# Output stage of a hybrid decoder layer: product order 7, 1, 6, 5, 3, 2, 4 with shared banks, three w_out sums made earlier, all sums on VectorE

## The chip, the cores and the metric

The kernel runs on one core of a Trainium2 chip. The metric is the device time of one execution in microseconds. The kernel before takes 1931.66 us, the median of three runs (1928.71 to 1932.95). The inputs are one sequence of 1024 tokens with a model width of 2048, in fp32.

## The reference

One layer, cut to its steps; `concat` is 2048 wide, and so is the output.

```python
h = rms_norm(x, norm_gain) * (1 + scale) + shift        # (1024, 2048)
proj = h @ w_in                                         # (2048, 8192): q k v z twice
oa = stick_breaking_attention(rms(qa), rms(ka), va) * silu(za)   # 8 heads of 128
ob = head_group_norm(chunkwise_retention(rotary(qr), rotary(kr), vr)) * silu(zr)
y = concatenate([oa, ob], -1) @ w_out                   # (2048, 2048)
out = x + gate * y
```

`scale`, `shift` and `gate` come from silu(c) @ w_ada + b_ada. The change concerns the last product, `concat @ w_out`, and what happens beside the input projection.

## The kernel before

**Arithmetic.** Every fp32 operand is cut in two: a high part (ScalarE's copy, L173 or L181) and a low part (VectorE's subtraction of the high part, L175 or L182). `mm3` then issues three matmuls for one product, high by high, high by low, low by high (L186 to L188). Both large products use Strassen's scheme in Winograd's form: 7 products of quarter matrices in place of 8, with sums of quarters ahead of and behind them.

**Groups.** The input projection runs in seven groups (0 to 6), each of 7 products in the order T4, B11, T2, T1, B22, B21, T3 (in groups 1 and later), named after their right factor. The left operands (`A`, w_in) are loaded raw (L260), summed on VectorE (L296) and cut (L173, L175); the right factors were cut once, in group 0, lie in DRAM (`fac`), and come back through a ring of buffers (L273, L275). One product of a group takes some 28 us. Between the matmuls of the projection small generators run a step at each tick: stick-breaking attention beside groups 1 to 4, retention beside groups 5 and 6, and two that only prepare something, `gate_steps` and `bias_steps` (the latter yields 6 ticks and 2 ticks in turn for each of its loads).

**Output stage** (L1424 and behind). The left matrix is `concat` turned (features by tokens), the right one w_out; each quarter product gives 512 by 1024 results, which is 4 token tiles by 2 halves of 512 columns `m`, and so all 8 PSUM banks, one tile `y` each. The inner dimension has 8 chunks `k` of 128. `steps` lists (product, halves, k): product 1 goes first with one half at a time (16 steps), then 7, 2, 6, 5, 3, 4 with both halves (8 steps each), 64 steps in all. A step has 24 matmuls (12 in the first 16 steps); the steps k=6 and k=7 of a product are issued together, bank by bank, and behind each bank the generator `later(1, ...)` puts its evacuation `evac_o` (L1618 to L1656). What multiplies results by the gate and adds x waits in a queue `fin`, from which one or two operations are taken at a time. Ahead of a step i, the right quarters of step i+6 are loaded (`load_right`), those of step i+5 summed where a product needs a sum (`sum_right`, GpSimd, L1474), and those of step i+3 cut. Sums of left quarters (`left_sum`, L1504 to L1516) stand on GpSimd as well. T3 (of product 7) and T2 (of product 6) are stored to DRAM once made (`sums_o`, L1483), and loaded again for the product behind (`load_s`, L1441).

**Order.** All of it runs in the order in which it is written out. SP issues every load and every store in that order, so a store that waits for its result holds back the loads behind it. The four evacuations of a product with most work are those of 6 and 5, L1628 and L1629, and L1631 to L1643; those of 3 are L1646 and the `fin` operations L1609 and L1613; those of 4 are L1653 and L1654.

Of the kernel before, what the change touches and what calls it, by code (L numbers as in the profile page):

```python
# [17 lines left out]
P = 128  # L18
# [80 lines left out]
def layer_kernel(ctx, tc, x, c, w_ada, b_ada, norm_gain, w_in, sb_q_gain, sb_k_gain, ret_norm_gain, w_out,  # L99
# [21 lines left out]
    sums_o = {(n, k): dr.tile([P, S], F32, name=f"sum_{n}_{k}") for n in ("T3", "T2") for k in range(8)}  # L121
# [729 lines left out]
    def bias_steps():  # L851

        acc = {}
        for i in range(2):
            n = min(HALF, NZ * P - i * HALF)
            acc[i] = get(f"qb_acc{i}", "att", borrow=True)
            for kc in range(KC):
                raw = get(f"wb_{kc}_{i}", "att", borrow=True)
                nc.sync.dma_start(raw[:, 0:n], w_in[0][kc * P:(kc + 1) * P, rqcol + i * HALF:rqcol + i * HALF + n])
                yield 6  # L860
                a, r, by = acc[i][:, 0:n], raw[:, 0:n], shift[:, kc:kc + 1]
# [6 lines left out]
        while clock[0] < scored[0] + 2:  # L868
            yield 1
        zs = ps.tile([P, NZ], F32, tag="A0", name="zs")  # L870
        for h in range(NZ):
            nc.tensor.matmul(zs[:, h:h + 1], acc[h // 4][:, h % 4 * P:(h % 4 + 1) * P], ones[:, 0:1],
                             start=True, stop=True)
        nc.vector.tensor_copy(qb[:, 0, 0:NZ], zs)
        put(acc[0], acc[1])
        yield 2
        nc.scalar.activation(qb[0:64, 1, 0:NZ], qb[64:128, 0, 0:NZ], AF.Copy)
        nc.scalar.activation(qb[64:128, 1, 0:NZ], qb[0:64, 0, 0:NZ], AF.Copy)
# [53 lines left out]
    def next_bank():  # L932
        turn_of[0] += 1
        return ("A0", "A1", "B", "C")[turn_of[0] % 4]

# [488 lines left out]
    steps = [(1, (m,), k) for m in range(2) for k in range(8)]  # L1424
    steps += [(prod, (0, 1), k) for prod in (7, 2, 6, 5, 3, 4) for k in range(8)]
    rraw, rcut, lraw, lcut, X, Y, gates, xrs = {}, {}, {}, {}, {}, {}, {}, {}
# [23 lines left out]
    def load_right(i):  # L1450
# [15 lines left out]
    def sum_right(i):  # L1466

        if i >= len(steps):
            return
        prod, ms, k = steps[i]  # L1470
        for m in ms:
            if len(rraw[i, m]) == 2:
                a, b = rraw[i, m]
                nc.gpsimd.tensor_tensor(a, a, b, op=ALU.add if prod == 6 else ALU.subtract)  # L1474
                put(b)

    def cut_right(i, m):
        if i >= len(steps) or m not in steps[i][1]:
            return
        prod, ms, k = steps[i]  # L1480
# [6 lines left out]
    def cut_left(i):  # L1487
# [3 lines left out]
        b = {1: "A11", 7: "S3", 2: "A12", 6: "A11", 5: "A21", 3: "A12", 4: "A22"}[prod]  # L1491
        t = lraw.pop(k) if prod == 7 else A_[b][k]
        lcut[i] = split(t, f"l{i}")
        if prod in (7, 5, 3, 4):
            put(t)
# [7 lines left out]
    def left_sum(n, k):  # L1503

        if n == "S3":
            t = lraw[k] = anywhere(f"S3o_{k}")
            nc.gpsimd.tensor_tensor(t, A_["A11"][k], A_["A21"][k], op=ALU.subtract)
        elif n == "S1":
            nc.sync.dma_start(concat[8 + k][:, halves(1)], A_["A22"][k])
            nc.gpsimd.tensor_tensor(A_["A21"][k], A_["A21"][k], A_["A22"][k], op=ALU.add)  # L1510
            put(A_["A22"].pop(k))
        elif n == "S2":
            nc.gpsimd.tensor_tensor(A_["A11"][k], A_["A21"][k], A_["A11"][k], op=ALU.subtract)
        else:
            nc.gpsimd.tensor_tensor(A_["A12"][k], A_["A12"][k], A_["A11"][k], op=ALU.subtract)
            put(A_["A11"].pop(k))  # L1516
# [18 lines left out]
    LOADS, SUMS, CUTS = 6, 5, 3  # L1535
    for k in range(8):
        at(6 + k, load_a, "A21", k)
        at(11 + k, left_sum, "S3", k)
        at(16 + k, load_a, "A12", k)
        at(19 + k, times_z, "A12", k)  # L1540
        at(18 + k, load_a, "A22", k)
        at(21 + k, times_z, "A22", k)
        at(22 + k, left_sum, "S1", k)
        at(27 + k, left_sum, "S2", k)
        at(33 + k, left_sum, "S4", k)
# [11 lines left out]
    for j in range(len(entries)):  # L1557
# [25 lines left out]
        if 3 <= left_over <= 8:  # L1583
            load_a("A11", 8 - left_over)
            load_right(8 - left_over)
        if left_over <= 3:
# [19 lines left out]
    def queue_out(t, n, y_):  # L1606

        load_xr(t, n)
        fin.append(lambda: nc.vector.tensor_tensor(y_, y_, gates[n], op=ALU.mult))  # L1609
# [8 lines left out]
    def evac_o(prod, b, o):  # L1618
        if prod in (1, 7):
# [3 lines left out]
        elif prod == 2:  # L1623
            y_ = anywhere(f"yt_{prod}_{b}")
            nc.vector.tensor_tensor(y_, o, X[b], op=ALU.add)
            queue_out(*where(prod, b), y_)
        elif prod == 6:
            nc.vector.tensor_tensor(X[b], o, X[b], op=ALU.add)  # L1628
            later(1, lambda: nc.vector.tensor_tensor(Y[b], X[b], Y[b], op=ALU.add))  # L1629
        elif prod == 5:  # L1630
            nc.vector.tensor_tensor(X[b], o, X[b], op=ALU.add)  # L1631
            y_ = anywhere(f"yt_{prod}_{b}")
            nc.vector.tensor_tensor(y_, o, Y[b], op=ALU.add)
            queue_out(*where(prod, b), y_)
            t, n = where(4, b)
            load_xr(t, n)
            fin.append(lambda: nc.vector.tensor_tensor(Y[b], Y[b], gates[n], op=ALU.mult))

            def add_x():
                x_ = xrs.pop((t, n))  # L1640
                nc.vector.tensor_tensor(Y[b], Y[b], x_, op=ALU.add)
                put(x_)
            fin.append(add_x)  # L1643
        elif prod == 3:
            y_ = X.pop(b)
            nc.vector.tensor_tensor(y_, o, y_, op=ALU.add)  # L1646
            queue_out(*where(prod, b), y_)
        else:
            y_, (t, n) = anywhere(f"yt_{prod}_{b}"), where(prod, b)
            for i, eng in enumerate((nc.sync, nc.scalar) if b == 7 else (nc.sync,)):  # L1650
# [3 lines left out]
                nc.vector.tensor_tensor(y_[:, sl], y_[:, sl], Y[b][:, sl], op=ALU.add)  # L1654
                eng.dma_start(out[0][t * P:(t + 1) * P, n * HALF + i * w:n * HALF + (i + 1) * w], y_[:, sl])
            put(y_, Y.pop(b))  # L1656
# [29 lines left out]
    for i, (prod, ms, k) in enumerate(steps):  # L1686
# [8 lines left out]
        for d in range(2 if both else 1):  # L1695
            load_right(i + d + LOADS)
            sum_right(i + d + SUMS)
            if i + d < 2:
                load_a("A11", i + d + LOADS)
# [24 lines left out]
        for d in range(2 if both else 1):  # L1724
            lcut.pop(i + d)
# [55 lines left out]
```

## Time and profile before

| | |
|---|---|
| median of three runs | 1931.66 us (1928.71 to 1932.95) |
| the profiled execution: its own time | 1935.53 us |
| the profiled execution: its span | 1933.8 us |
| granted TensorE clock, mean over the span | 0.993 |
| output stage, first matmul of `y` to the end of the span | 1598.8 to 1933.8 us |
| GpSimd, busy over the span | 254.4 us of 1933.8, 374 instructions |

The span is what the profile sees of the execution; its own time is 1.7 us longer. The profiled execution lies 3.9 us above the median. In a table of windows each row is a stretch of the span: first its length, then the busy time of PE, PEld (TensorE's weight loads), DVE (VectorE), ACT (ScalarE) and POOL (GpSimd) with the number of instructions in brackets, then the TensorE clock that was granted (1.00 is full), the busy share of the DMA engines and GB/s. A matmul of 512 columns shows 0.39 us in the records, but one starts every 0.227 us: the records overlap, so that a busy time near the window's length says little, and the number of matmuls in a window says more. The same holds for VectorE, whose records of 0.68 us start 0.60 us apart. A row of a timeline has the start, the duration, the engine, the line, the result and its operands, and in square brackets the idle time ahead of it and what ended that.

### The profile page before, as it was taken

The page shows a single profiled execution, that of the slowest core. Times are in us where ns is not written, and L with a number is a line of the kernel's source. Part 1 is how long each engine was busy: PE and PEld are TensorE (multiplying, and loading weights), DVE is VectorE, ACT ScalarE, POOL GpSimd, SP SyncE. Part 2 cuts the span into 40 slices and gives each one's busy share as a digit, 9 for nine tenths or more (in the row PEclk, how much of TensorE's full clock was granted, in tenths as well). Part 3 has the DMA queues.
Part 4 walks back from the last instruction along what each step waited for, and adds up shares of the span by engine and source line. Part 5 has one row for each costly group of instructions (what it writes and reads, how often), then busy time and mean ns, then how long its engine had stood idle before and what let it go on. Part 6 is the DMA issues. An engine that isn't in the chain of part 4 may idle for free.

```text
span 1933.8 us, 28606 instructions
## 1 busy us (share of the span) xinstructions
PE 1877.2 (97%) x9511; PEld 1538.1 (80%) x9511; DVE 1377.4 (71%) x2522; ACT 839.7 (43%) x1574; POOL 254.4 (13%) x374
## 2 busy tenths in 40 slices
PE   5999999999999999999999999999999999998988
PEld 3777778878788878887888788888888888886777
DVE  4637765447768777877787667966786657898797
ACT  5437852234544454445444444333343546422221
POOL 0000000000110011001000100000000003597232
PEclk9999999999999999999999999999999999999999
DMA  9969996897798779977997788989988847988574
GB/s 319 361 206 315 322 339 244 284 354 250 245 302 281 255 255 318 312 259 241 310 299 260 255 264 277 296 255 315 343 290 243 273 144 255 327 295 278 161 254 160
DMA packets 407216, 532.62 MB, mean 275 GB/s; under 512 B 33566, under 2 KB 207000, under 8 KB 407068
## 3 DMA queue, kind: packets, MB, share of 16 engines
q1 hardware_dynamic: 406536, 530.62, 83.2%
q8 instruction: 75, 1.23, 0.3%
q14 instruction: 73, 0.60, 0.1%
q10 hardware_dynamic: 532, 0.17, 0.0%
HBM read 444.64 MB, written 86.02 MB: 274 GB/s over the span
## 4 chain that ended last, share of the span: by engine, by line
PE 42%; DVE 6%; DMA 3%; issue 1%; SPq 0%; ACT 0%; POOL 0%; DVEq 0%; POOLq 0%
PE pj L186 8%; PE pj L188 8%; PE pj L187 8%; PE y L186 3%; PE y L187 3%; PE y L188 3%; DMA wB<-in_w_out_dram 1%; PE op L1321 1%; PE sp L1305 1%; PE op L1323 1%; PE up L1287 1%; DVE wl_l L175 1%; DVE r_1l L182 0%; DVE Y L1629 0%; DVE yt L1609 0%
## 5 line engine op out<-in xcount | busy, mean ns | idle before, releaser
L175 DVE TENSOR_TENSOR wl<-A,wh 128x512 fp32r<-128x512 f32 x392 | 272.1, 694 | 274.9 <-ACT wh L173 251.8
L173 ACT ACTIVATE wh<-A 128x512 fp32r<-128x512 f32 x392 | 246.7, 629 | 358.9 <-PE pj L187 341.7
L1086 POOL TENSOR_SCALAR_AFFINE_SELECT om<-om 128x128 f32<-128x128 f32 x64 | 25.5, 398 | 1073.8 <-ACT om L1083 936.6
L389 ACT ACTIVATE c<-pj 128x512 f32<-128x512 f32 x112 | 66.5, 598 | 183.5 <-PE pj L188 144.7
L392 DVE TENSOR_TENSOR c<-pj,c 128x512 f32<-128x512 f32 x112 | 74.9, 687 | 67.0 <-PE pj L188 66.8
L296 DVE TENSOR_TENSOR A<-A,A 128x512 f32<-128x512 f32 x160 | 109.9, 694 | 1.7
L186 PE MATMUL y<-r_0h,wh_l 128*128 128x512 f32 x224 | 89.1, 398 | 7.8 <-DVE X L1628 6.1
L186 PE MATMUL y<-r_1h,wh_l 128*128 128x512 f32 x224 | 89.2, 398 | 5.8 <-DVE X L1646 4.7
L1099 DVE TENSOR_TENSOR_SCAN om<-om 128x128 f32<-128x128 f32 (+2 forms) x96 | 93.7, 976 | 1.1
L186 PE MATMUL first<-h_hi,wh_first 128*128 128x512 f32 x224 | 92.4, 412 | 1.1 <-ACT h_hi L596 1.1
L186 PE MATMUL pj<-T1h,wh 128*128 128x512 f32 x232 | 92.5, 399 | 0.0
L186 PE MATMUL pj<-B21h,wh 128*128 128x512 f32 x232 | 92.3, 398 | 0.0
L186 PE MATMUL pj<-B22h,wh 128*128 128x512 f32 x232 | 92.3, 398 | 0.0
L186 PE MATMUL pj<-B11h,wh 128*128 128x512 f32 x232 | 91.7, 395 | 0.0
L188 PE MATMUL pj<-B21h,wl 128*128 128x512 f32 x232 | 90.9, 392 | 0.0
L188 PE MATMUL pj<-T1h,wl 128*128 128x512 f32 x232 | 90.7, 391 | 0.0
L188 PE MATMUL pj<-B22h,wl 128*128 128x512 f32 x232 | 90.7, 391 | 0.0
L188 PE MATMUL pj<-T3h,wl 128*128 128x512 f32 x224 | 88.8, 397 | 1.8 <-DVE wl L175 1.8
L187 PE MATMUL pj<-B21l,wh 128*128 128x512 f32 x232 | 90.6, 390 | 0.0
L187 PE MATMUL pj<-T1l,wh 128*128 128x512 f32 x232 | 90.6, 390 | 0.0
L187 PE MATMUL pj<-B22l,wh 128*128 128x512 f32 x232 | 90.5, 390 | 0.0
L188 PE MATMUL pj<-B11h,wl 128*128 128x512 f32 x232 | 90.5, 390 | 0.0
(280 smaller groups left out, 5216.4 us busy)
## 6 DMA issues: line engine op xcount, KB each, us to landing
A<-in_w_in_dram SPq DMA_DIRECT2D x228, 256.0 KB, 5.4
wB<-in_w_out_dram SPq DMA_DIRECT2D x144, 256.0 KB, 5.5
ada<-in_w_ada_dram SPq DMA_DIRECT2D x128, 256.0 KB, 5.7
gr<-in_w_ada_dram SPq DMA_DIRECT2D x64, 256.0 KB, 5.5
T2h<-fac_T SPq DMA_DIRECT2D x56, 256.0 KB, 5.2
T2l<-fac_T SPq DMA_DIRECT2D x56, 256.0 KB, 5.3
T1h<-fac_T SPq DMA_DIRECT2D x56, 256.0 KB, 4.8
T1l<-fac_T SPq DMA_DIRECT2D x56, 256.0 KB, 5.1
```

What stands on the lines that cost most here:

```text
L173: nc.scalar.activation(hi[:, 0:n], src[:, 0:n], AF.Copy)
L175: nc.vector.tensor_tensor(lo[:, 0:n], src[:, 0:n], hi[:, 0:n].bitcast(F32), op=ALU.subtract)
L186: nc.tensor.matmul(o, a_hi, b_hi, start=first, stop=False, skip_group_check=on)
L187: nc.tensor.matmul(o, a_hi, b_lo, start=False, stop=False, skip_group_check=on)
L188: nc.tensor.matmul(o, a_lo, b_hi, start=False, stop=last, skip_group_check=on)
L296: nc.vector.tensor_tensor(r[o], r[a], r[b], op=ALU.add if n == 1 else ALU.subtract)
L389: nc.scalar.activation(t, o, AF.Copy)
L392: nc.vector.tensor_tensor(dst[q, cc], o, dst[q, cc], op=ALU.add)
L1086: nc.gpsimd.affine_select(om[:, n - P:n], om[:, n - P:n], pattern=[[-1, P]], compare_op=ALU.is_gt, fill=1.0, base=0, channel_multiplier=1)
L1099: nc.vector.tensor_tensor_scan(rev, rev, rev, init, op0=ALU.mult, op1=ALU.bypass)
L1287: nc.tensor.matmul(up[:, j * P:(j + 1) * P], kd[:, j * P:(j + 1) * P], vb(4 * g + j), start=True, stop=True)
L1305: nc.tensor.matmul(sp[:, j, :], r["k", g][:, tk], r["q", g][:, tk], start=True, stop=True)
```

## The change

The output stage goes through the products in the order 7, 1, 6, 5, 3, 2, 4; now product 7 is the one that runs one half at a time, and its cut left operands serve both halves.

Products 1, 6, 5 and 3 accumulate in the same 8 banks: only product 1 starts a bank afresh, and each evacuation reads the running sum. So 6 needs one VectorE operation for a bank (V = o + Y, L1651), 5 and 2 one and the gate and x, 3 a multiplication straight from the bank and an addition, 4 what it had.

The sums T3 = B22 - B12, T1 = B12 - B11 and T2 of w_out's quarters are made in `sum_steps` (L938), a generator that follows `bias_steps` from group 3 on; `bias_steps` yields 4 and 1 ticks where it yielded 6 and 2. For each of 16 pieces `sum_steps` loads three quarters, makes three sums on VectorE and stores them: 48 loads (L946), 48 sums (L950) and 48 stores (L952) in all, 6 transfers in every 18 ticks. As the program is written out, 16 of the 96 lie in group 3 behind its product T1, some 33 are passed in group 4, some 35 in group 5, and the rest in group 6 beside T4. The output stage then loads one stored sum for products 7, 6 and 5.

Product 4's sum and all sums of left quarters go from GpSimd to VectorE. The counts of the output stage, from the instructions as they are written out: GpSimd 96 operations before and none now; VectorE 340 and 351 (evacuations and `fin` operations 128 and 104); transfers 317 and 246; matmuls 1344 and 1344.

GpSimd at the border of the last group and the output stage, before (a row has the line, the operation, the result and its operands, numbered by buffer); `rq` and `dm` are retention's, `wB22`, `wB12` quarters of w_out, `S3o` a left sum:

```order
L1311 TENSOR_TENSOR rq_7_0_16882<-rq_7_0_16882,dm_7_17186 128x512
L1311 TENSOR_TENSOR rq_7_1_17002<-rq_7_1_17002,dm_7_17186 128x512
L1474 TENSOR_TENSOR wB22_0_0_17824<-wB22_0_0_17824,wB12_0_0_17826 128x512
L1474 TENSOR_TENSOR wB22_0_1_17828<-wB22_0_1_17828,wB12_0_1_17830 128x512
L1507 TENSOR_TENSOR S3o_0_17864<-A11o_0_17264,A21o_0_17716 128x512
L1474 TENSOR_TENSOR wB22_1_0_17854<-wB22_1_0_17854,wB12_1_0_17856 128x512
L1474 TENSOR_TENSOR wB22_1_1_17858<-wB22_1_1_17858,wB12_1_1_17860 128x512
L1507 TENSOR_TENSOR S3o_1_17898<-A11o_1_17293,A21o_1_17720 128x512
```

The same place now:

```order
L1331 TENSOR_TENSOR rq_6_0_16645<-rq_6_0_16645,dm_6_16957 128x512
L1331 TENSOR_TENSOR rq_6_1_16763<-rq_6_1_16763,dm_6_16957 128x512
L1331 TENSOR_TENSOR rq_7_0_17086<-rq_7_0_17086,dm_7_17390 128x512
L1331 TENSOR_TENSOR rq_7_1_17206<-rq_7_1_17206,dm_7_17390 128x512
L1801 UNCONDITIONAL_BRANCH
L1801 ISA
```

Behind retention's last operation GpSimd had 96 more; now it has only the program's end.

VectorE at the evacuation of product 6, before; `y` are the banks, X and Y running results in SBUF, `r_0l` and `wl_l` low parts:

```order
L1628 TENSOR_TENSOR X_17729<-y_0_18911,X_17729 128x512
L175 TENSOR_TENSOR wl_l_19276<-A21o_17720,wh_l_19274 128x512
L1629 TENSOR_TENSOR Y_18402<-X_17729,Y_18402 128x512
L1628 TENSOR_TENSOR X_17741<-y_1_18920,X_17741 128x512
L182 TENSOR_TENSOR r_1l<-wB_1_1_19094,r_1h 128x512
L1629 TENSOR_TENSOR Y_18414<-X_17741,Y_18414 128x512
L1628 TENSOR_TENSOR X_17754<-y_2_18930,X_17754 128x512
L1629 TENSOR_TENSOR Y_18426<-X_17754,Y_18426 128x512
L1628 TENSOR_TENSOR X_17762<-y_3_18939,X_17762 128x512
L1629 TENSOR_TENSOR Y_18434<-X_17762,Y_18434 128x512
```

The same place now:

```order
L1651 TENSOR_TENSOR V_18907<-y_0_18210,Y_17949 128x512
L175 TENSOR_TENSOR wl_l_18917<-A21o_18098,wh_l_18915 128x512
L1651 TENSOR_TENSOR V_18919<-y_1_18218,Y_17957 128x512
L182 TENSOR_TENSOR r_1l<-wT_1_1_18765,r_1h 128x512
L1651 TENSOR_TENSOR V_18931<-y_2_18226,Y_17970 128x512
L1651 TENSOR_TENSOR V_18939<-y_3_18234,Y_17978 128x512
L1651 TENSOR_TENSOR V_18947<-y_4_18242,Y_18163 128x512
L1651 TENSOR_TENSOR V_18955<-y_5_18250,Y_18175 128x512
```

Of two operations for a bank one is left, and it does not depend on another evacuation.

SP in group 5 near a load of retention's mask `dm`, before; T3 and T4 are ring loads, `A` are raw pieces of w_in, `pr_rk` and `pr_rv` are stores of a projection's results:

```order
L273 DMA T3h_6_15166<-fac_T_6_228 128x512
L275 DMA T3l_6_15168<-fac_T_6_228 128x512
L273 DMA T3h_7_15170<-fac_T_7_229 128x512
L275 DMA T3l_7_15172<-fac_T_7_229 128x512
L260 DMA A_6_3_1_15184<-in_w_in_dram 128x4x128
L1255 DMA dm_15186<-in_ret_mask_dram 128x256
L260 DMA A_6_0_0_15219<-in_w_in_dram 128x4x128
L402 DMA pr_rk_138<-c_5_0_13972 128x512
L260 DMA A_6_1_0_15257<-in_w_in_dram 128x4x128
L402 DMA pr_rv_146<-c_5_1_14011 128x512
```

The same place now:

```order
L273 DMA T3h_6_15352<-fac_T_6_236 128x512
L275 DMA T3l_6_15354<-fac_T_6_236 128x512
L260 DMA A_6_3_1_15367<-in_w_in_dram 128x4x128
L1275 DMA dm_15369<-in_ret_mask_dram 128x256
L952 DMA sum_T_7_181<-sB_7_0_15232 128x512
L260 DMA A_6_0_0_15403<-in_w_in_dram 128x4x128
L402 DMA pr_rk_138<-c_5_0_14115 128x512
L260 DMA A_6_1_0_15442<-in_w_in_dram 128x4x128
L402 DMA pr_rv_146<-c_5_1_14155 128x512
L952 DMA sum_T_7_165<-sB_7_0_15234 128x512
```

Among the same loads there stand stores of sums (`sum_T`) from `sB` now, and loads of `sB` a little further ahead; each store waits for a sum on VectorE.

The diff, cut:

```diff
     def bias_steps():
...
-                yield 6
+                yield 4
...
-                yield 2
...
+                yield 1
...
+        yield from sum_steps()
...
+    def sum_steps():
+
+        for k in range(8):
+            for m in range(2):
+                B = {}
+                for n in ("B22", "B12", "B11"):
+                    f, c_ = k + 8 * (n[1] == "2"), m + 2 * (n[2] == "2")
+                    B[n] = get(f"s{n}_{k}_{m}", "att", borrow=True)
+                    nc.sync.dma_start(B[n], w_out[0][f * P:(f + 1) * P, halves(c_)])
+                yield 6
+                for n, o, a, b, op in (("T3", "B22", "B22", "B12", ALU.subtract),
+                                       ("T1", "B12", "B12", "B11", ALU.subtract), ("T2", "B11", "B22", "B11", ALU.add)):
+                    nc.vector.tensor_tensor(B[o], B[a], B[b], op=op)
+                    yield 2
+                    nc.sync.dma_start(sums_o[n, k][:, halves(m)], B[o])
+                    yield 2
+                put(*B.values())
...
-    steps = [(1, (m,), k) for m in range(2) for k in range(8)]
-    steps += [(prod, (0, 1), k) for prod in (7, 2, 6, 5, 3, 4) for k in range(8)]
+    steps = [(7, (m,), k) for m in range(2) for k in range(8)]
+    steps += [(prod, (0, 1), k) for prod in (1, 6, 5, 3, 2, 4) for k in range(8)]
...
-            elif prod == 7:
-                rraw[i, m] = [load_b("B22", k, m), load_b("B12", k, m)]
-            elif prod == 6:
-                rraw[i, m] = [load_s("T3", k, m), load_b("B11", k, m)]
-            elif prod == 5:
-                rraw[i, m] = [load_b("B12", k, m), load_b("B11", k, m)]
+            elif prod == 4:
+                rraw[i, m] = [load_b("B21", k, m), load_s("T2", k, m)]
             else:
-                rraw[i, m] = [load_b("B21", k, m), load_s("T2", k, m)]
...
+                rraw[i, m] = [load_s({5: "T1", 6: "T2", 7: "T3"}[prod], k, m)]
...
-                nc.gpsimd.tensor_tensor(a, a, b, op=ALU.add if prod == 6 else ALU.subtract)
-                put(b)
...
+            nc.vector.tensor_tensor(a, a, b, op=ALU.subtract)
+            put(b)
...
-        if prod in (7, 6):
-            nc.sync.dma_start(sums_o["T3" if prod == 7 else "T2", k][:, halves(m)], t)
...
+                lcut[i] = lcut[i + 8] = split_to(t, f"l{i}", "any")
...
-            nc.gpsimd.tensor_tensor(A_["A21"][k], A_["A21"][k], A_["A22"][k], op=ALU.add)
+            nc.vector.tensor_tensor(A_["A21"][k], A_["A21"][k], A_["A22"][k], op=ALU.add)
...
-    LOADS, SUMS, CUTS = 6, 5, 3
+    LOADS, SUMS, CUTS = 6, 4, 3
...
         elif prod == 6:
-            nc.vector.tensor_tensor(X[b], o, X[b], op=ALU.add)
-            later(1, lambda: nc.vector.tensor_tensor(Y[b], X[b], Y[b], op=ALU.add))
-        elif prod == 5:
-            nc.vector.tensor_tensor(X[b], o, X[b], op=ALU.add)
...
+            V[b] = anywhere(f"V_{b}")
+            nc.vector.tensor_tensor(V[b], o, Y[b], op=ALU.add)
+        elif prod in (5, 2):
+            y_ = (Y if prod == 5 else X).pop(b)
             nc.vector.tensor_tensor(y_, o, y_, op=ALU.add)
             queue_out(*where(prod, b), y_)
...
+        elif prod == 3:
+            y_, (t, n) = anywhere(f"yt_{prod}_{b}"), where(prod, b)
+            nc.vector.tensor_tensor(y_, o, gates[n], op=ALU.mult)
+            queue_out(t, n, y_, False)
...
-                if k == 0:
-                    tag, bufs = ("pj", 4) if prod == 1 else tags[b]
+                if k == 0 and prod not in (6, 5, 3):
+                    tag, bufs = ("pj", 4) if prod == 7 else tags[b]
...
-                    mm3(out_banks[b], l[0][:, tk], l[1][:, tk], r[0], r[1], k + d == 0, k + d == 7)
+                    mm3(out_banks[b], l[0][:, tk], l[1][:, tk], r[0], r[1], k + d == 0 and prod not in (6, 5, 3),
+                        k + d == 7, True)
...
-                    if t % 2 and prod != 6:
+                    if t % 2:
```

More of the change, by code (lines that the diff above doesn't have):

```diff
@@ L120, in layer_kernel @@
     krow = [dr.tile([1, S], F32, name=f"krow{h}") for h in range(NH)]
[L121 removed]
+    sums_o = {(n, k): dr.tile([P, S], F32, name=f"sum_{n}_{k}") for n in ("T1", "T2", "T3") for k in range(8)}
     fac = {(n, k): dr.tile([P, 2, HALF], F32, name=f"fac_{n}_{k}") for n in RIGHT.values() for k in range(8)}
@@ L866, in bias_steps @@
                 put(raw)
-                yield 2
[L868 to L875, printed above, removed]
+                yield 1
+            while clock[0] < scored[0] + 2:
+                yield 1
+            hs = slice(4 * i, min(NZ, 4 * i + 4))
+            zs = ps.tile([P, NZ], F32, tag="A0", name=f"zs_{i}")
+            for h in range(hs.start, hs.stop):
+                nc.tensor.matmul(zs[:, h:h + 1], acc[:, h % 4 * P:(h % 4 + 1) * P], ones[:, 0:1],
+                                 start=True, stop=True)
+            nc.vector.tensor_copy(qb[:, 0, hs], zs[:, hs])
+            put(acc)
+            yield 2
+            nc.scalar.activation(qb[0:64, 1, hs], qb[64:128, 0, hs], AF.Copy)
+            nc.scalar.activation(qb[64:128, 1, hs], qb[0:64, 0, hs], AF.Copy)
         yield 2
-        nc.scalar.activation(qb[0:64, 1, 0:NZ], qb[64:128, 0, 0:NZ], AF.Copy)
-        nc.scalar.activation(qb[64:128, 1, 0:NZ], qb[0:64, 0, 0:NZ], AF.Copy)
+        yield from sum_steps()
     def gate_steps():
@@ L1724, in layer_kernel @@
         for d in range(2 if both else 1):
-            lcut.pop(i + d)
+            parts = lcut.pop(i + d)
+            if 8 <= i + d < 16:
+                put(*parts)
             for m in ms:
```

107 lines of the change are left out of this document (53 added, 54 removed).

## The prediction

> **What bounds the kernel now.** I read the page's first lines, then the tile `y` of the output stage, then windows over its 335 us and over the groups, and last the waits and timelines where a window fell short.
>
> ```profile
> span 1933.8 us, 28606 instructions
> PE 1877.2 (97%) x9511; PEld 1538.1 (80%) x9511; DVE 1377.4 (71%) x2522; ACT 839.7 (43%) x1574; POOL 254.4 (13%) x374
> L186 PE MATMUL y<-r_0h,wh_l x224: 388/389/797, 1598.8 to 1922.8; 128*128 128x512 f32 x112
> L188 PE MATMUL y<-r_1h,wl_l x224: 388/389/632, 1622.1 to 1928.6; 128*128 128x512 f32 x112
> ```
>
> TensorE is the bound, 97% busy. The change leaves its matmuls as they are, so only its gaps can be won or added. The pace without gaps comes from two starts 12 matmuls apart, in group 5:
>
> ```profile
> 1382.03 0.39 PE L186 MATMUL pj<-T3h,wh 128*128 128x512 f32 x1
> 1383.85 0.39 PE L188 MATMUL pj<-T3h,wl 128*128 128x512 f32 x1
> 1384.75 0.39 PE L186 MATMUL pj<-T3h,wh 128*128 128x512 f32 x1
> ```
>
> (1384.75 - 1382.03) / 12 = 0.227 us for one. The output stage's 1344 need 305 us; their rows reach from 1598.8 to 1929.0, which is 330. Windows show where the rest lies (PE, PEld, DVE, ACT, POOL, clock, DMA share, GB/s):
>
> ```profile
> 1650.00:1700.00 50.00, 50.00 (x222) 41.43 (x221) 44.62 (x49) 21.10 (x38) 25.58 (x15) 1.00 0.94 320
> 1700.00:1750.00 50.00, 49.88 (x220) 40.94 (x219) 48.77 (x41) 12.99 (x23) 50.00 (x28) 1.00 0.83 285
> 1750.00:1800.00 50.00, 41.49 (x159) 30.40 (x158) 44.59 (x47) 12.94 (x23) 38.88 (x25) 0.90 0.74 252
> 1800.00:1850.00 50.00, 50.00 (x222) 41.43 (x221) 39.16 (x64) 16.02 (x30) 0.79 (x1) 1.00 0.57 178
> 1850.00:1900.00 50.00, 43.64 (x181) 34.80 (x180) 45.43 (x61) 11.69 (x21) 23.87 (x13) 0.93 0.83 275
> ```
>
> A full window has 222 matmuls. Two fall short, by 63 and by 41: 104 x 0.227 = 23.6 us. The first is the end of product 6, the second that of product 3. What TensorE waited for there (us in all, times, longest), and the worst 10 us of each:
>
> ```profile
> PE y L186 <- DVE X L1628: 7.0, 5, 2.3
> PE y L186 <- DVE X L1646: 6.4, 4, 4.7
> 1780.00:1790.00 10.00, 6.40 (x12) 3.33 (x12) 9.90 (x11) 2.41 (x4) 10.00 (x7) 0.55 0.94 321
> 1880.00:1890.00 10.00, 5.30 (x16) 3.95 (x15) 5.64 (x11) 0.63 (x1) 3.90 (x4) 0.67 0.87 271
> ```
>
> TensorE waits for VectorE's evacuations, and the granted clock then falls to 0.55 and 0.67. In the first, VectorE is busy 9.90 of 10 us with only 11 operations, beside a GpSimd that is never idle. The timelines of both engines at 1706, and of VectorE alone at 1844, say why:
>
> ```profile
> 1706.21 1.78 DVE L175 TENSOR_TENSOR wl_l<-A12o,wh_l 128x512 fp32r<-128x512 f32 x1
> 1707.91 1.77 DVE L182 TENSOR_TENSOR r_1l<-wB,r_1h 128x512 fp32r<-128x512 f32 x1
> 1707.40 1.73 POOL L1513 TENSOR_TENSOR A11o<-A21o,A11o 128x512 f32<-128x512 f32 x1
> 1709.10 1.74 POOL L1510 TENSOR_TENSOR A21o<-A21o,A22o 128x512 f32<-128x512 f32 x1
> 1844.21 0.68 DVE L1613 TENSOR_TENSOR yt<-yt,xr 128x512 f32<-128x512 f32 x1
> 1844.82 0.68 DVE L1637 TENSOR_TENSOR Y<-Y,gb 128x512 f32<-128x512 f32 x1
> ```
>
> Beside GpSimd both engines go in step, one operation in 1.70 us each; alone, VectorE starts one every 0.60 us. So each of the 96 GpSimd sums that meets VectorE costs it one operation of 1.1 us more. The second stop also has a load in it (VectorE's row, then SP's issue):
>
> ```profile
> 1884.54 0.69 DVE L1613 TENSOR_TENSOR X<-X,xr 128x512 f32<-128x512 f32 x1 [4.36 <-DMA xr<-in_x_dram]
> 1879.12 3.01 SPq L1600 DMA_DIRECT2D xr<-in_x_dram  x5
> ```
>
> VectorE stood 4.36 us for x, whose load SP issued only at 1879: SP works in order and stands at stores of results that a late VectorE has not made.
>
> **The change, part by part. GpSimd's sums.** All 96 go: 32 left sums and 16 sums of product 4 move to VectorE in this stage, 48 move into the groups. Its evacuations and `fin` operations fall from 128 to 104, and 8 left cuts go: 340 operations before, 351 now. At 0.60 us these are 211 us in 305. One product of 192 matmuls lasts 43.5 us and holds 72 operations of 0.60 us; the fullest, the last, has about 73 ahead of its final evacuations by the order of the instructions, 43.8 us. VectorE thus keeps up, with no more than 1 us over.
>
> **The banks.** Products 6, 5 and 3 add into the banks of the product before, which costs no matmul. Their k=0 still waits for the evacuation of the same bank, as it did. For product 6 one VectorE operation per bank replaces a chain of two, so the end of product 6, today's worst place, has 8 operations fewer. I take all 23.6 us as won and put back 2 us for borders at which x or a store is late, between 0 (no wait is left) and 9 us (a stop like that at 1880 stays: 41 x 0.227 = 9.3).
>
> **Transfers of the stage** fall from 317 to 246 at 256 KB each. That is cover, not time: the windows with no gap show 0.57 to 0.94 of DMA share. **The end** is the same: the last evacuations of product 4 stay four small operations.
>
> **The groups.** `sum_steps` adds 48 VectorE sums, 48 loads and 48 stores from group 3 on. These windows lie in groups 4 to 6:
>
> ```profile
> 1200.00:1250.00 50.00, 49.69 (x252) 41.33 (x251) 47.93 (x79) 17.31 (x31) 1.85 (x2) 1.00 0.89 291
> 1300.00:1350.00 50.00, 50.00 (x275) 42.92 (x274) 32.39 (x77) 19.73 (x37) 2.59 (x2) 1.00 1.05 315
> 1350.00:1400.00 50.00, 49.12 (x240) 41.09 (x239) 32.84 (x79) 18.42 (x34) 1.30 (x1) 1.00 1.05 337
> 1211.00:1400.00 189.00, 188.00 (x974) 159.19 (x973) 137.97 (x302) 69.28 (x126) 9.50 (x7) 1.00 0.96 301
> 1400.00:1430.00 30.00, 30.00 (x165) 25.24 (x164) 25.73 (x52) 10.24 (x18) 1.29 (x1) 1.00 1.04 355
> ```
>
> VectorE: 48 x 0.60 = 29 us over some 500 us, hidden wherever it has room. Only at T4 (1200 to 1250) is it nearly full, 47.93 of 50; some 6 sums there are 3.6 us with 2 us of room, and the 1.6 us that are left shift low parts (`wl`) that lie some us ahead of TensorE. This comes in groups 4 and 5.
>
> Transfers: about 35 pass in group 5, 35 x 0.262 MB = 9.2 MB, or 49 GB/s over its 189 us, on top of 301. The total, 350 GB/s, is above the 337 of the busiest 50 us and below the 355 of the busiest 30 us here. At 337 the backlog is (350 - 337) x 189 us = 2.5 MB or 7 us; at 355 it is nothing. What a backlog of 7 us delays is read here, SP's issue of a ring load and the first matmul with it, and the mask of retention:
>
> ```profile
> 1319.49 0.84 SPq L273 DMA_DIRECT2D B21h<-fac_B  x1
> 1349.64 0.48 PE L186 MATMUL pj<-B21h,wh 128*128 128x512 f32 x1
> SPq L273 <- PE pj L188: 17.1, 6, 6.6
> 1379.42 0.69 DVE L1310 TENSOR_TENSOR pT<-sp,dm 128x512 f32<-128x512 f32 x1 [6.09 <-DMA dm<-in_ret_mask_dram]
> 1380.63 0.77 DVE L175 TENSOR_TENSOR wl<-A,wh 128x512 fp32r<-128x512 f32 x1
> ```
>
> Ring loads are issued 30 us ahead of use and land in about 5, and SP itself stood 17.1 us for the ring's buffers between 1240 and 1300, so up to then it has free time to give. The mask is the weak spot: VectorE stands 6.09 us for it already, and the `wl` behind it ends at 1381.40, 2.5 us ahead of its matmul at 1383.85. Each us beyond that stops TensorE. Of a 7 us lag, 4.5 us are then paid at one head; at the other heads, where the wait is short now, most is absorbed. I take 4 us for the groups, between 0 and 12.
>
> The Trainium skill, "DMA: Bandwidth & Descriptors", section "Specifications", gives about 358 GB/s as the HBM limit of one core. By it 350 would just fit and the groups would cost nothing, 4 us less in the sum; the 355 GB/s of 1400 to 1430 agree with it, the 337 at a share of 1.05 show that mixed traffic can stay below.
>
> The same source, "TensorE: Matmul & The Clock Gate", section "What's actually happening", says that after an idle window of some 3.4 us the clock is halved until TensorE was busy for as long. The 0.55 agrees. By it a new stop in the groups would cost more than its own length, which speaks against the change; the sum would stay at 1914 as long as each stop is short, as the forecast has it.
>
> **Sum:** 1931.7 - 23.6 + 2 + 4 = 1914. Against the profiled execution (1935.5, span 1933.8) it is the same 17.6 us less: a span of about 1916. I subtract from the median, since the gaps come from the order of the program and not from that one execution.
>
> **Rivals.**
>
> A. *The groups pay more, 12 us.* Retention's loads come late at several heads: each of five heads between 1230 and 1430 loses 2.5 us. For it: the 6.09 us above, a DMA share of 1.05, VectorE full at T4. Against it: TensorE lost only 1 us of 189 there, and 17.1 us of SP's time are free. 1914 + 8 = 1922.
>
> B. *The other side: transfers are not absorbed.* Where the queue is full, each added transfer takes 0.262 MB / 337 GB/s = 0.8 us; if group 5 has no room for its 35, the backlog is 28 us. It decides once it passes the ring's lead, 30 - 5 = 25 us, or if VectorE waits for masks by all of it: TensorE then stops for up to 28 us. For it: the share of 1.05 for 100 us on end. Against it: 0.83 to 0.89 shares before 1300 and 0.86 after 1400. 1914 - 4 + 28 = 1938, slower.
>
> C. *Stops in the output stage stay.* The wait for x at a product's border comes from issue order, not from GpSimd; it may appear at products 5, 3 and 2, as product 3 now adds x directly behind its evacuation. 9.3 us stay: 1914 + 8 = 1922, or 1930 at two borders. Against it: SP's lateness came from stores of a late VectorE, and transfers fall by 71. If VectorE's long operations did not come from GpSimd, nothing would be won here either; but at 1844, with GpSimd idle, it runs 0.60.
>
> **How the numbers follow.** Forecast 0.64, A 0.14, B 0.10, C 0.12. The forecast's own range is 1906 (0 in the groups, 0 at the borders, and 2 us of clock) to 1920. To leave out no more than 2 in 10 it takes in A and the smaller C: 1906 to 1927. A measurement of this kernel tells about 0.2%, 3.9 us, from no change. Below 1927.8: the forecast, A and most of C, 0.83. Between: part of C and of a mild B, 0.05. Above 1935.5: most of B and the rest, 0.12.
>
> **What would show it.** Right: GpSimd empty behind about 1640; VectorE's operations 0.60 us apart through the stage; 220 matmuls or more in each 50 us of it, at a clock of 1.00; the stage's rows some 22 us shorter; the first `y` matmul 0 to 8 us later than 1598.8. Rival A shows as waits of VectorE for `dm`, `rk` or `rq` and of TensorE for `wl` in groups 5 and 6. B shows as TensorE waiting for ring loads. C shows as TensorE waiting for VectorE at 43.5 us intervals, with VectorE behind `xr`. The prediction is wrong if the first `y` matmul comes over 12 us late, or if windows of the stage still fall short.

## The result, and the profile after

The changed kernel takes 1936.5 us (median of 20 runs, 1932.4 to 1943.5) against 1934.1 us before (20 runs): a ratio of 1.0018, with a 95% interval of 1.0008 to 1.0028. Forecast were 1914 us and a range of 1906 to 1927, subtracted from three runs whose median lay 2.4 us below that of these 20. The output stage brought what was forecast, and the groups took all of it back.

The first lines of the page of the changed kernel:

```profile
span 1940.5 us, 28542 instructions
PE 1876.2 (97%) x9511; PEld 1541.4 (79%) x9511; DVE 1334.2 (69%) x2587; ACT 833.7 (43%) x1568; POOL 86.2 (4%) x278
```

TensorE is busy as long as before, GpSimd for 86 us in place of 254, and the span is 6.7 us longer. Each trace is of one execution: that of the change took 1942.3 us, 5.7 above its median, and that of before 1935.5 us, 1.4 above its own, so that differences between these two traces are some 4 us larger than between the medians. Windows of the changed kernel, three of the output stage and three of groups 5 and 6, with the columns of the prediction:

```profile
1700.00:1750.00 50.00, 50.00 (x222) 41.44 (x221) 30.82 (x51) 19.52 (x35) 0.00 (x0) 1.00 0.37 126
1750.00:1800.00 50.00, 50.00 (x222) 41.40 (x221) 26.73 (x43) 15.20 (x27) 0.00 (x0) 1.00 0.31 100
1850.00:1900.00 50.00, 50.00 (x222) 41.44 (x221) 36.32 (x60) 15.05 (x27) 0.00 (x0) 1.00 0.97 325
1300.00:1350.00 50.00, 40.54 (x214) 34.80 (x213) 28.22 (x71) 15.76 (x30) 1.29 (x1) 0.90 0.87 272
1350.00:1400.00 50.00, 44.96 (x226) 37.60 (x226) 31.19 (x74) 16.97 (x32) 2.86 (x2) 0.93 1.03 331
1450.00:1500.00 50.00, 46.16 (x233) 38.58 (x232) 38.36 (x94) 18.37 (x34) 3.01 (x2) 0.93 0.74 236
```

The output stage now has its 222 matmuls in every window, where the same windows had 159 and 181. The windows of retention, which were full, now hold 214, 226 and 233 matmuls, and the clock falls to 0.90. The borders of the stages, read from the first T4 matmul of groups 5 and 6 and the first `y` matmul of the changed kernel:

```profile
1216.57 0.39 PE L186 MATMUL pj<-T4h,wh 128*128 128x512 f32 x1
1423.46 0.39 PE L186 MATMUL pj<-T4h,wh 128*128 128x512 f32 x1
1629.30 0.48 PE L186 MATMUL y<-r_0h,l0h 128*128 128x512 f32 x1
```

Such rows of each run give its stages, in us (group: from its first T4 matmul to the next one's, or to the first `y`; output: from there to the end of the span). Single executions scatter: the change, e1, e2, e3, e4, e8 and e12 issue the same work in group 2 and take 204.0 to 208.2 us there:

| run | group 2 | 3 | 4 | 5 | 6 | output |
|---|---|---|---|---|---|---|
| before | 199.6 | 199.1 | 201.3 | 188.1 | 199.1 | 335.0 |
| the change | 204.0 | 200.2 | 200.0 | 206.9 | 205.8 | 311.2 |
| e1 no sums in the groups | 207.8 | 203.1 | 199.4 | 188.9 | 199.1 | 311.2 |
| e2 buffers alone | 206.8 | 200.2 | 199.4 | 201.1 | 199.1 | 311.2 |
| e3 `on` given back later | 208.2 | 200.2 | 202.0 | 198.7 | 205.3 | 311.2 |
| e4 transfers alone | 205.3 | 204.9 | 200.8 | 196.8 | 210.2 | 311.2 |
| e5 no sums, old bias steps | 198.9 | 199.1 | 201.3 | 188.1 | 199.1 | 311.3 |
| e6 sums from group 1 | 208.6 | 208.5 | 201.3 | 188.4 | 199.1 | 311.2 |
| e8 without the VectorE sums | 204.0 | 200.0 | 199.3 | 201.0 | 207.3 | 311.3 |
| e9 all sums in the output stage, VectorE | 200.3 | 199.0 | 201.3 | 189.2 | 199.1 | 318.4 |
| e10 the same on GpSimd | 199.2 | 199.0 | 201.2 | 188.3 | 199.1 | 327.5 |
| e11 before, its sums on VectorE | 199.1 | 200.5 | 201.3 | 189.3 | 199.1 | 323.6 |
| e12 sums' transfers on GpSimd's queue | 206.4 | 200.2 | 201.6 | 209.8 | 205.8 | 311.3 |
| e13 as e9, gate rows later | 199.9 | 199.3 | 201.3 | 188.8 | 199.1 | 311.4 |
| e14 as e5, bias steps closer | 202.5 | 204.7 | 199.4 | 189.3 | 199.1 | 311.3 |

The output stage is 23.8 us shorter; the first `y` matmul comes 30.5 us later: 4.9 us by the start of group 5, 18.8 us in group 5, 6.7 us in group 6 (with rounding).

What waits there in the changed kernel, from the waits of groups 5 and 6, ScalarE's of group 5 alone (us in all, times, longest). `state` is what retention carries on from chunk to chunk of a head, `on` a head's result on its way to `concat`, `rk` and `sw_k` its keys, and `c` a result of the projection:

```profile
PE op L1343 <- DVE state L1317: 18.2, 3, 9.5
ACT on L1348 <- DMA concat<-on: 15.4, 1, 15.4
ACT c L389 <- DMA pr_rk<-c: 10.5, 1, 10.5
DVE pT L1330 <- DMA dm<-in_ret_mask_dram: 11.9, 4, 5.7
DVE sw_k L1253 <- DMA sw_k<-pr_rk: 8.4, 2, 6.7
```

The same waits before:

```profile
PE op L1323 <- DVE state L1297: 0.9, 1, 0.9
ACT c L389 <- DMA pr_rk<-c: 6.5, 1, 6.5
DVE pT L1310 <- DMA dm<-in_ret_mask_dram: 6.6, 2, 6.1
DVE sw_k L1233 <- DMA sw_k<-pr_rk: 2.6, 1, 2.6
```

The longest of the three stops, in rows of SP, ScalarE, VectorE and TensorE:

```profile
1321.65 0.46 SPq L1383 DMA_DIRECT2D concat<-on  x1
1327.26 0.60 ACT L1348 ACTIVATE on<-op 128x512 f32<-128x512 f32 x1 [15.42 <-DMA concat<-on]
1327.89 0.89 DVE L1351 BATCH_NORM_STATS2 st<-op 128x6 f32<-128x128 f32 x4 [10.43 <-ACT on L1348]
1332.09 0.92 DVE L1317 SCALAR_TENSOR_TENSOR state<-state,up 128x128 f32<-128x128 f32 x3
1332.42 0.79 PE L1343 MATMUL op<-state,rq 128*128 128x128 f32 x2 [9.46 <-DVE state L1317]
```

Read from the bottom: TensorE needs retention's `state`, which VectorE makes in order behind the statistics of `on`; these wait for ScalarE's copy into `on` (L1348); and this copy waits 15.42 us for a store, since it goes into the buffer that head 0's `on` still occupies. Nothing computed in the waiting chain is late by itself. The other two stops have other waits ahead of `state`: ScalarE stands 10.48 us for a store of `rk`, and VectorE 6.72 us for a load of `sw_k`:

```profile
1372.14 0.60 ACT L389 ACTIVATE c<-pj 128x512 f32<-128x512 f32 x1 [10.48 <-DMA pr_rk<-c]
1382.19 0.80 PE L1343 MATMUL op<-state,rq 128*128 128x128 f32 x2 [4.91 <-DVE state L1317]
1442.02 0.69 DVE L1253 TENSOR_TENSOR sw_k<-sw_k,sin 128x512 f32<-128x512 f32 x1 [6.72 <-DMA sw_k<-pr_rk]
1456.52 0.80 PE L1343 MATMUL op<-state,rq 128*128 128x128 f32 x2 [3.84 <-DVE state L1317]
```

Why the copy of the first stop meets that store can be read off the program's own hand-out of buffers, which takes the one free longest (tile, its buffer, that buffer's last tile, buffers free in the class, requests and returns since it came back):

```
before   on_1_0  buffer 87  last sw_k2_0  free 6  29
change   on_1_0  buffer 36  last on_0_0   free 4   7
```

`sum_steps` holds three buffers of that class. Fewer are free, so a buffer goes round sooner, and head 1's `on` gets the one from which head 0's is being stored.

### The profile page after: what moved, and what is told of

Its sections match the earlier page's. It is cut to its first block, busy times and chain, and to the rows that moved or that the text cites. A ratio compares the mean times of both kernels' runs of the same rounds, so it can differ in the third digit from the quotient of the medians.

```text
span 1940.5 us, 28542 instructions
## 1 busy us (share of the span) xinstructions
PE 1876.2 (97%) x9511; PEld 1541.4 (79%) x9511; DVE 1334.2 (69%) x2587; ACT 833.7 (43%) x1568; POOL 86.2 (4%) x278
## 4 chain that ended last, share of the span: by engine, by line
PE 43%; DVE 4%; DMA 4%; issue 0%; ACT 0%; SPq 0%; DVEq 0%; ACTq 0%
PE pj L186 8%; PE pj L187 8%; PE pj L188 8%; PE y L186 4%; PE y L187 4%; PE y L188 4%; DMA sw_q<-rqraw 1%; DMA sw_k<-pr_rk 1%; PE op L1343 1%; PE op L1341 1%; DVE wl L175 1%; PE sp L1325 1%; DMA xr<-in_x_dram 1%; PE up L1307 0%; PE oT L188 0%
## 5 line engine op out<-in xcount | busy, mean ns | idle before, releaser
L187 PE MATMUL pj<-B11l,wh 128*128 128x512 f32 x232 | 91.0, 392 | 0.0
L186 PE MATMUL pj<-T4h,wh 128*128 128x512 f32 x224 | 89.6, 400 | 0.0
L186 PE MATMUL pj<-T3h,wh 128*128 128x512 f32 x224 | 88.7, 396 | 0.9 <-ACT wh L173 0.9
```

Source lines behind the costliest of these rows:

```text
L186: nc.tensor.matmul(o, a_hi, b_hi, start=first, stop=False, skip_group_check=on)
L187: nc.tensor.matmul(o, a_hi, b_lo, start=False, stop=False, skip_group_check=on)
```

## The experiments

Two theories at the start. **Q**: the 96 transfers make SP's queue late, and with it retention's loads and stores. **B**: the three buffers make others come round too soon. Ratios are to the kernel before.

**e1, no sums in the groups.** `sum_steps` is not run; products 7, 6 and 5, and product 4 for its second operand, load plain quarters, so that the kernel leaves out the sums of `sum_steps`.

```diff
-        yield from sum_steps()
...
-                rraw[i, m] = [load_s({5: "T1", 6: "T2", 7: "T3"}[prod], k, m)]
+                rraw[i, m] = [load_b({5: "B12", 6: "B11", 7: "B22"}[prod], k, m)]
```

> Leaves out the w_out sums in the groups (no buffers, no transfers, no VectorE sums); the output stage loads plain quarters of w_out in place of the stored sums, so its result is not the reference's. Theory Q (96 more transfers make SP's queue late) and theory B (three more buffers taken from the pool of attention and retention tiles make a buffer come round too soon, so that retention's `on` waits for a store) both expect the whole loss of groups 5 and 6 (18.8 + 6.7 us) to go and the gain of the output stage (23.8 us) to stay: about 1911 us, with some 5 us of loss left in group 2 that comes from the denser bias steps. A rival that puts the loss down to something else in the change expects 1930 or more.

1919.9 us, 0.9927 (0.9904 to 0.9949). Groups 5 and 6 are back at 188.9 and 199.1 us: the sums cost 1936.5 - 1919.9 = 16.7 us. The time lies 9 us above the expected 1911: more than the expected 5 us is left in groups 2 and 3, where e1's trace has 8.2 and 4.0 us more than before.

**e2, the buffers alone.** `sum_steps` takes and returns them at the same ticks, with no load, sum or store.

```diff
-                    nc.sync.dma_start(B[n], w_out[0][f * P:(f + 1) * P, halves(c_)])
...
-                    nc.vector.tensor_tensor(B[o], B[a], B[b], op=op)
...
-                    nc.sync.dma_start(sums_o[n, k][:, halves(m)], B[o])
...
```

> The buffers alone: sum_steps takes its three buffers and gives them back at the same ticks, but moves and sums nothing (the output stage loads plain quarters; result not the reference's). B expects `on` of head 1 to wait for the store of `on` of head 0 again, by 5 us or more, and a time of 1920 to 1932. Q expects 1911, as with no sums at all.

1926.8 us, 0.9959 (0.9945 to 0.9973): 6.9 us above e1. The waits of e2 show the same copy behind the same store, with no transfer added:

```profile
ACT on L1344 <- DMA concat<-on: 14.0, 1, 14.0
PE op L1339 <- DVE state L1313: 10.6, 2, 8.0
```

B holds for that stop: holding three buffers, and doing nothing with them, makes it. By the traces it costs group 5 more than 6.9 us, namely 201.1 - 188.9 = 12.2 us, while group 3 takes 2.9 us less than in e1. The five runs that hold the buffers beside the new bias steps (the change, e2, e3, e8, e12) take 200.0 to 200.2 us in group 3, and the three that do not (e1, e4, e14) 203.1 to 204.9. So the 6.9 us are a net figure; why group 3 gains was not tried.

**e3, another buffer for head 1's `on`.** The changed kernel with one line moved.

```diff
-                put(on)
+                later(6, lambda: put(on))
```

> The change as it is, but retention's `on` buffer is given back 6 ticks later, so that head 1's `on` takes another buffer. Everything is computed. B expects TensorE's wait of 9.5 us at 1322 and the low clock behind it to go: 1922 to 1928. Q expects no more than 2 us: 1934 to 1937.

1931.5 us, 0.9982 (0.9964 to 1.0001): 5 us below the change, less than B expected, more than Q. The execution in the trace took 1937.0 us, among the longest of ten (1925.6 to 1937.1). The wait for `concat<-on` is gone and group 5 takes 198.7 us, but the wait of ScalarE for a store of `rk` and of VectorE for the mask grew (e3's waits):

```profile
ACT c L389 <- DMA pr_rk<-c: 14.0, 1, 14.0
DVE pT L1330 <- DMA dm<-in_ret_mask_dram: 14.5, 3, 9.4
```

**e4, the transfers alone.** 96 copies from DRAM to DRAM in the same places, with no buffer and no sum.

```diff
-                    B[n] = get(f"s{n}_{k}_{m}", "att", borrow=True)
-                    nc.sync.dma_start(B[n], w_out[0][f * P:(f + 1) * P, halves(c_)])
+                    B[n] = w_out[0][f * P:(f + 1) * P, halves(c_)]
+                    nc.sync.dma_start(sums_p[n, k][:, halves(m)], B[n])
...
-                    nc.vector.tensor_tensor(B[o], B[a], B[b], op=op)
...
```

> The transfers alone: at the places of the 48 loads and 48 stores, 96 copies of a quarter piece from DRAM to DRAM (as many bytes through the queue, twice the HBM traffic), with no buffer taken and no sum made; the output stage loads plain quarters; result not the reference's. Q expects the loss to stay or grow: 1930 to 1945, with SP's loads of group 5 late. B expects 1911 to 1918.

1940.8 us, 1.0029 (1.0016 to 1.0042): 20.9 us above e1. No wait for `concat<-on` is left, but (waits of e4):

```profile
DVE pT L1329 <- DMA dm<-in_ret_mask_dram: 21.5, 4, 9.0
ACT c L390 <- DMA pr_rk<-c: 13.2, 1, 13.2
```

The transfers stop retention by themselves. By the pages e4 reads and writes 25.2 MB of HBM each above e1, the change 12.6 MB each, so the 20.9 us may lie above what the real transfers cost; no run has these alone. Q and B are both at work.

**e5, the old bias steps.** e1 with `bias_steps` of the kernel before.

> As e1_no_sums (no w_out sums, plain quarters in the output stage, result not the reference's), with the bias steps of the kernel before (6 and 2 ticks, one `zs` at the end). If the denser bias steps with their `zs` matmuls in the middle of groups 2 and 3 cost what group 2 lacks (207.8 us in e1 against 199.6), that group is back at 199 to 201 us and the time is 1909 to 1914. If group 2's loss has another cause, it stays: 1918 to 1922.

1910.8 us, 0.9874 (0.9855 to 0.9892). Every group takes what it took before, to 0.7 us, and only the output stage differs. So the denser bias steps cost 1919.9 - 1910.8 = 9.1 us where no sums stand behind them. They also sum up in two groups of small matmuls, `zs`, where the old ones have one at their end. **e14** is e5 with the closer pace but one `zs`:

```diff
-                yield 6
+                yield 4
...
-                yield 2
+                yield 1
```

> e5 (old bias steps, no w_out sums, plain quarters; result not the reference's) with the bias steps at 4 and 1 ticks, but still one `zs` at their end. If the closer loads cost group 2 its 8 us, they are back: 1917 to 1922. If it is the `zs` in the middle of group 2, waiting for ScalarE, 1909 to 1914.

1916.9 us, 0.9908 (0.9888 to 0.9928): of the 9.1 us, some 6 are the pace. The other 3 may be the two `zs`, which e1 has besides, but the intervals of e1 and e14 overlap, so that this part is not shown.

**e6, the sums from group 1 on,** with the old bias steps.

```diff
+            if gi == 1:
+                run_apart(sum_steps())
```

> The change with everything computed, but sum_steps starts in group 1, beside the gate and the old bias steps, and is done before retention begins. Transfers, VectorE sums and buffers are the same in number. The theory that it is retention's place (groups 5 and 6 at a full DMA queue and with few free buffers) that makes the sums dear expects 1909 to 1916, with 188 us for group 5 and 199 for group 6. The rival that 96 transfers and three buffers cost about as much anywhere expects 1922 or more.

1932.8 us, 0.9985 (0.9975 to 0.9995): if retention's place were the cause, 1909 to 1916 were expected, and by its rival 1922 or more. Groups 5 and 6 are free of loss, but groups 2 and 3 take 9 us more each. A window of group 2, and what ScalarE and TensorE waited for from 735 to 800, in e6:

```profile
750.00:800.00 50.00, 44.41 (x218) 36.81 (x218) 32.24 (x59) 20.27 (x42) 5.81 (x24) 0.97 0.95 317
ACT c L389 <- DMA pr_k<-c: 7.8, 1, 7.8
PE zp L186 <- ACT be L1102: 3.0, 1, 3.0
```

In the same stretch before, ScalarE also waited for such a store, 6.3 us, but TensorE waited only 0.5 us for ScalarE's `be`. The rival was right: attention's groups pay for the sums as retention's do. Which of their waits carries the 9 us is not shown.

**e8, without the 48 sums on VectorE** (`nc.vector.tensor_tensor(B[o], ...)` left out of `sum_steps`).

> The change without the 48 sums on VectorE: each loaded quarter is stored as it is, so a store waits for its load alone and not for VectorE (result not the reference's). If the sums or the stores that stand in SP's queue for them carry part of the loss, the time falls by 4 us or more, to 1926 to 1932. If transfers and buffers carry it all, it stays at 1934 to 1938.

1934.2 us, 0.9988 (0.9976 to 1.0000): 2.4 us below the change by the medians, some 6 us by the ratios to the kernel before (0.9988 against 1.0018), whose median was 1934.1 to 1936.3 us from one set of runs to the next. The sums on VectorE, with the waits of the stores for them, carry a small part, of uncertain size.

**e12, the sums' transfers on GpSimd's queue** (`nc.gpsimd.dma_start` for the 48 loads and 48 stores).

> The change with everything computed, but the 48 loads and 48 stores of the sums are issued by GpSimd on its own queue, so they do not stand in SP's order; buffers, sums and bytes are the same. If SP's order is what makes retention's loads and stores late, 8 us or more come back: 1920 to 1928. If it is the bytes and the buffers, 1933 to 1940.

1946.4 us, 1.0060 (1.0037 to 1.0083): slower than both kernels, and above the 1933 to 1940 that were expected if bytes and buffers are the cause. ScalarE's wait for `concat<-on` is still there, 16.3 us. But GpSimd, which also multiplies retention's `rq` by the mask, now stands in order for VectorE's sums ahead of their stores (e12's waits from 900 to 1640):

```profile
POOL sum_T L952 <- DVE sB L950: 242.8, 31, 18.8
```

So taking these transfers out of SP's order gives nothing back. Since they then stand in another engine's order, the run does not tell how much of their price SP's order makes.

**The output stage, taken apart: e9, e10, e11.** e9 has the new order and banks, but makes all sums in the stage, T3, T2 and T1 too, on VectorE; e10 makes the same sums on GpSimd; e11 is the kernel before with its 96 sums on VectorE. All three have the old bias steps. The cut shows lines of e9 and e11 against the kernel before:

```diff
             elif prod == 7:
                 rraw[i, m] = [load_b("B22", k, m), load_b("B12", k, m)]
...
-                nc.gpsimd.tensor_tensor(a, a, b, op=ALU.add if prod == 6 else ALU.subtract)
+                nc.vector.tensor_tensor(a, a, b, op=ALU.add if prod == 6 else ALU.subtract)
```

> Everything computed. The new product order and shared banks, all sums on VectorE, but none in the groups: T3, T2, T1 are made in the output stage from pairs of loads as the kernel before made them, on VectorE in place of GpSimd (48 more VectorE operations over products 7, 6 and 5), and the bias steps are those of the kernel before. If the output stage's gain needs only a VectorE free of GpSimd and of chained evacuations, and VectorE has room for 16 more operations a product (51 operations in 50 us of after, some 82 fit at 0.60 us), then 1910 to 1915. If VectorE becomes the bound of the stage: 1918 to 1930.

> As e9, but all 96 sums of the output stage on GpSimd, as in the kernel before. If GpSimd's lockstep with VectorE (1.70 us for an operation in place of 0.60) made the stage's stops, they come back: 10 us or more above e9. If the shared banks and single evacuations alone do it, within 3 us of e9.

> The kernel before with nothing changed but the engine of its 96 output sums, VectorE in place of GpSimd. If the lockstep is the whole cause, the stage loses its 23 us of stops: 1910 to 1914. If the product order and chained evacuations matter by themselves, a stop stays at the end of product 6 or 3: 1915 to 1930.

e9 1918.3 us, 0.9911 (0.9889 to 0.9933); e10 1926.1 us, 0.9949 (0.9927 to 0.9970); e11 1922.7 us, 0.9933 (0.9911 to 0.9954). The stage takes 318.4, 327.5 and 323.6 us, against 335.0. e10 lies 7.9 us above e9, between the two expectations; e9 lies where VectorE as the bound was expected, but by another cause, shown below; e11 lies where the order was expected to matter by itself. In e11, windows at the ends of products 6 and 3, and the waits:

```profile
1750.00:1800.00 50.00, 46.67 (x199) 36.44 (x198) 42.95 (x70) 13.75 (x25) 0.00 (x0) 1.00 0.83 286
1850.00:1900.00 50.00, 46.02 (x188) 36.78 (x187) 43.10 (x71) 12.18 (x22) 0.00 (x0) 0.93 0.75 250
PE y L186 <- DVE X L1646: 4.0, 3, 3.1
PE y L186 <- DVE X L1628: 3.3, 7, 0.8
```

Without GpSimd the old order still stops at both places, less long. In e10 VectorE is back at one operation in 1.70 us (starts at 1701.67 and 1703.36), and a window holds 182 matmuls:

```profile
1700.00:1750.00 50.00, 45.07 (x182) 35.86 (x183) 50.00 (x38) 12.06 (x22) 48.76 (x30) 0.93 0.68 228
1701.67 1.77 DVE L1507 TENSOR_TENSOR A12o<-A12o,c 128x512 f32<-128x512 f32 x1
1703.36 1.77 DVE L182 TENSOR_TENSOR r_0l<-wT,r_0h 128x512 fp32r<-128x512 f32 x1
```

So the engine alone is worth 11.4 us of the stage, the order alone 7.5, and both together, in the change, 23.8. e9 keeps one stop. Its window, and VectorE's waits of the stage's first 100 us, in e9:

```profile
1650.00:1700.00 50.00, 45.94 (x191) 37.31 (x190) 33.87 (x57) 17.20 (x31) 0.00 (x0) 0.93 1.02 368
DVE gb L1533 <- DMA bb<-in_b_ada_dram: 16.1, 3, 9.3
```

VectorE stands in order at an addition for the gate, whose result is first used at 1772, behind a full DMA queue. **e13** moves it:

```diff
-        at(17 + n, load_gate, n)
+        at(28 + n, load_gate, n)
```

> e9 with one move: the gate's rows and their additions stand at steps 28 to 31 in place of 17 to 20. Everything is computed. In e9 the stage had one stop, at 1690, where VectorE stood 16.1 us for the bias rows of the gate behind a DMA queue at a share of 1.02. If that is the cause, the stop goes and the time is 1909 to 1914. If VectorE's own load or the right quarters are late there, 1916 to 1920.

1911.0 us, 0.9875 (0.9854 to 0.9896). The window of e13 has its matmuls, at the same DMA share:

```profile
1650.00:1700.00 50.00, 50.00 (x222) 41.44 (x221) 43.24 (x72) 19.69 (x36) 0.00 (x0) 1.00 1.03 375
```

This version beats both kernels: it takes 23.5 us, 1.25%, less than before. It has the change's product order, banks and engine, and nothing of it in the groups.

## Why the prediction was wrong

**The output stage: right in size, half right in cause.** Forecast were 23.6 us won and 2 us put back; measured were 23.8 us. VectorE's pace of 0.60 us and the 222 matmuls a window came as said, and no wait for x is left, so rival C did not come (its sum should have added 9.3 - 2 = 7.3 us, not 8, which changes nothing). But the working put the stops down to GpSimd's lockstep, with the banks as a help at product 6 only. Against the 311.4 us of e13's stage, which makes the same sums, e11 shows that VectorE with the old order still loses 12.2 us, and e10 that the new order beside GpSimd loses 16.1, of which up to 7.0 can be e9's stop at the gate's rows, since e10 has them at the same place. That the size came out is in part luck: the change moved the sums and changed the order at once, and the working gave nearly the whole to the first.

**The groups: wrong, 4 us forecast and 30.5 measured in the trace, some 26 by the medians** (1936.5 - 1934.1 + 23.8). A first `y` matmul over 12 us late was the prediction's own sign of being wrong. Three steps failed.

The step that failed most is the one on what a backlog delays. It followed the ring loads and one mask load, gave each its lead, and took the rest for absorbed. It never asked where the three `sB` buffers come from. With them, head 1's `on` waits for a store that is issued 10 us after the wait begins (1327.26 - 15.42 = 1311.84, the issue 1321.65), and three engines in order stand behind it. e2 shows that the buffers alone cost 6.9 us net. The ring, on which the prediction spent its rows, was never waited for: rival B's size came nearly true, its mechanism did not.

The second is the transfers' term, taken as a lag of 7 us of which 4.5 are paid at one head. TensorE was stopped three times instead, and the waits of VectorE for `dm` rose from 6.6 to 11.9 us, those for `sw_k` from 2.6 to 8.4 us. That is rival A's mechanism; e4 shows that it stops retention without any buffer taken. Each stop also costs clock (0.90 and 0.93 in those windows), as the prediction's sentence on the Trainium skill's "TensorE: Matmul & The Clock Gate", section "What's actually happening", had it; the sum held nothing for it.

The third is a term that was left out. The bias steps' new pace stands in the change, and the prediction gave it neither a price nor a cover. It costs 9.1 us by the medians of e1 and e5, less in the change itself, where group 3 is back at 200.2 us.

By medians the whole reads: 1935.5 before, 24.7 us less for the output stage (e5), 9.1 us more for the bias steps (e1), 16.7 us more for the sums (the change), 1936.5. From the ratios the three terms are 24.4, 10.3 and 17.6 us; the medians are of different sets of runs. How the 16.7 us divide between bytes and buffers is not settled to the microsecond, since the parts overlap: 6.9 us for buffers alone, and e3, with that one stop removed, is still 11.6 us above e1.

## What to carry to other kernels

Work that is moved beside a busy stage takes buffers as well as engine time and bytes: look up, in the order in which buffers are handed out, which tile now gets whose buffer, and whether the last use of it is a store. Price every pace that is changed, also of steps that only make room. Before moving work out of a stage, see whether the stage has room once its stops are gone: here VectorE was busy for 27 to 36 us of 50 in the windows of the changed kernel, the sums fitted in, and one load at a full queue had to move.

## What had not been expected of the hardware

The same 96 transfers cost more when GpSimd issues them (1946.4 us) than in SP's order (1936.5 us), though GpSimd has only 86 us of other work. Its 242.8 us behind VectorE's sums may be why; this was not tried. And the queue goes higher than the 355 GB/s on which the prediction set its upper bound: 375 GB/s over 50 us in e13, with no stop of TensorE. The page of the kernel before already has a slice of 48 us at 361 GB/s. So 337 to 355 GB/s are no ceiling of the queue, though the transfers of group 5 are a different mix from these. The 375 GB/s also lie above the 358 GB/s that the prediction cites; here the measurement decides.
